# A hybrid encoder layer: another order for the output projection's first loads and the feed-forward's first splits, and up-projection weights moved by 64 bytes

## The chip, the cores and the metric

The kernel runs on one core of a Trainium2 chip. The metric is the device time of one execution in microseconds (us), from the runs of the whole program. A profile is one further execution, taken by the hardware profiler, with a time of its own. The engines are called PE (TensorE, matmuls), DVE (VectorE), ACT (ScalarE), POOL (GpSimd) and SP (SyncE, which here issues the loads). PEld is PE's weight load.

## The reference

One layer (DEPTH = 1) works on x of 512 rows and 1024 columns, all in float32:

```
h      = RMSNorm(x)
parts  = h @ w_in                      # pooling, attention, recurrence and three gates
y_pool = pool_mixer(...)               # 512 x 512 each
y_attn = diff_attention(...)
y_rec  = hgrn2_mixer(...)
merged = sigmoid(gate0) * (y_pool @ w_up_pool[l])
       + sigmoid(gate1) * (y_attn @ w_up_attn[l])
       + sigmoid(gate2) * (y_rec @ w_up_rec[l])
x      = x + merged @ w_out[l]
h2     = RMSNorm(x)
gu     = h2 @ w_ffn_in[l]
x      = x + (silu(gu[..., :2816]) * gu[..., 2816:]) @ w_ffn_out[l]
out    = RMSNorm(x)
```

The change touches the gates and up-projections of the last two branches (pooling, attention), the loads of w_out, and the first columns of w_ffn_in.

## The kernel before

**Products in three terms.** [...] Each weight block is split on the chip into a high part, `whi` (a cast on ACT, L183), and the rest, `wlo` (a subtraction on DVE, L184). The moving operand is split likewise, and a product is hi·hi + lo·hi + hi·lo. `split_w` does this for a block of 128 x 1024 (or 128 x 512) into a buffer of the pool `wsp`, which has three and a little room at the end of each: its argument `skip` puts the block `skip` bytes further on in the buffer.

**Half-size products.** For a pair of column blocks, a form with seven products of half size (256 columns) takes the place of eight: the "pairs". Of their weights, four parts are made: part 0 and part 3 are plain splits of the raw weights (whole, and half), parts 1 and 2 are splits of sums of raw weights. The sums are made by `PairChunk.add` on DVE (L261, L264, L265), their splits by L300 (`shi`, ACT) and L302 (`slo`, DVE). Five pairs of gate blocks (pooling 6, attention 0, 2, 4 and 6) and the pairs 1 to 21 of the feed-forward work this way; the gate pairs' plain parts have `skip=64`. A pair's body has four generators, `first` to `fourth`, one for each part; each issues its matmuls and what takes the results out of PSUM, such as `g` (L1250), `u` (L1255) and `hid` (L1261) in the feed-forward.

**What sets the order.** `Jobs` holds a list of jobs in order, each with its weight parts. `pump` looks ahead: it loads the next chunk of raw weights (about 1 MB, on SP's queue) as soon as fewer than two chunks of the pool `wraw` are still to be split, and splits the next part when fewer than `limit` (3, later 4) parts are held. A chunk with a `where` has a pool of its own instead: it waits until that pool is opened (`Chunk.ready`). `PairPart.ready` and `behind` add an order by hand: a pair's part isn't split before an event named in `after` has been issued, and its instructions stand behind that event's on their engines. The table `after` names events for pairs 1 to 3 alone: `forms_mid` and `forms_end` are points in the making of the moving operand's forms (sums of blocks of h2 and their splits, which need DVE too), `g1` is pair 1's addition into `g`, and `s12_2` is pair 2's first `slo`.

**The stages around the change.** After the pooling mixer come, in order: up-projections of the pooling branch and its gate pair 6; up-projections 6 and 7; attention gate pairs 0 and 2; up-projections 0 to 3; gate pairs 4 and 6; up-projections 4 to 7. Each up-projection of 128 columns has 12 matmuls of 512 columns; two of them share one weight part. Then x is loaded again (L1655, 2 MB), and the output projection begins: two `out_quarter_job`s, each 256 columns of w_out by four blocks of rows in matmuls of 256 columns, and one `out_last_job` with the other 512 columns, in matmuls of 512. The first megabyte of w_out (columns 0 to 255) goes to the pool `wx`, which is opened at L1650 (`LAST["wx"]`), when the gates' pool of forms has been closed. The norm and its transposes are woven in, and the feed-forward starts: pair 1's first part, the plain columns (`u0`, `g0`, L1209 and on), then pairs 1 to 21. In pair 4, two matmuls of 512 columns whose result isn't used stand behind the first part (L1222 and on), one reading its moving operand at the start of the weight buffer, the other 64 bytes further on.

Of the kernel before, what the change touches and what calls it, by code (L numbers as in the profile page):

```python
# [76 lines left out]
def encoder_kernel(ctx: ExitStack, tc: tile.TileContext, x, norm1_g, w_in, pool_w, pool_scale,  # L77
# [7 lines left out]
    def pool(name, bufs=1, **kw):  # L85
        return tc.tile_pool(name=name, bufs=bufs, **kw)
# [62 lines left out]
    LAST, FF = {}, {}  # L149
# [28 lines left out]
    def split_w(view, a, b, wpool=None, skip=0):  # L178

        n, k = a * b, skip // 4  # L180
        hi, lo = ((wpool or wsp).tile([P, n if wpool else 1088], F32R, name=name)[:, k:k + n]
                  .rearrange("p (a b) -> p a b", a=a) for name in ("whi", "wlo"))
        nc.scalar.copy(out=hi, in_=view)  # L183
        LAST["wlo"] = nc.vector.tensor_tensor(out=lo, in0=view, in1=hi.bitcast(F32), op=ALU.subtract).ins  # L184
        return hi, lo
# [46 lines left out]
    jobs = Jobs()  # L232
# [34 lines left out]
    @contextmanager  # L267
    def behind(after):

        with ExitStack() as st:  # L270
            for i in after:
                st.enter_context(tc.issue_after(i))
            yield

    class PairPart:
# [17 lines left out]
        def sums_and_split(self):  # L293
            k = KT // 2
            if self.which in (1, 2):
                if self.chunk.sums is None:
                    self.chunk.add()
                view = self.chunk.sums[:, 2:4] if self.which == 1 else self.chunk.sums[:, 0:2]
                hi = LAST["ws"].tile([P, 2, k * P], F32R, name="shi")
                nc.scalar.copy(out=hi, in_=view)  # L300
                lo = LAST["ws"].tile([P, 2, k * P], F32R, name="slo")
                on_dve = nc.vector.tensor_tensor(out=lo, in0=view, in1=hi.bitcast(F32), op=ALU.subtract).ins  # L302
                FF.setdefault(f"s12_{self.chunk.name}", (on_dve,))
            elif self.which == 0:
                hi, lo = split_w(self.chunk.raw[:, 0], KT, P, None, self.skip)
                hi, lo = (t.rearrange("p k c -> p (k c)").rearrange("p (n x) -> p n x", n=2) for t in (hi, lo))
            else:
                hi, lo = split_w(self.chunk.raw[:, 1, k:], k, P, None, self.skip)
                hi, lo = (t.rearrange("p k c -> p (k c)").rearrange("p (n x) -> p n x", n=1) for t in (hi, lo))
            self.hi, self.lo = (t.rearrange("p n (k c) -> p n k c", c=P) for t in (hi, lo))  # L310
            self.chunk.left -= 1
# [101 lines left out]
    def quarter_parts(w, c0, n, where=None, skip=0):  # L413

        v = w.rearrange("(kt p) c -> p kt c", p=P)
        for c in range(0, n, 256):
            ch = Chunk(v[:, :, c0 + c:c0 + c + 256], KT, 256, where if c == 0 else None)
            yield slice(c, c + 256), [Part(ch, lambda raw, j=j: raw[:, j:j + 4, :], 4, 256, None, skip)
                                       for j in (0, 4)]
# [57 lines left out]
    stA = ExitStack()  # L477
# [213 lines left out]
    def up_job(idx, dt, y, first, last_hl):  # L691
        def body(part):
            ps = bank("mm")
            yield from cols_mm(ps, part, y(), 4, dt % 2)
            sg = gate_sb.pop((idx, dt))
            if first:
                nc.vector.tensor_tensor(out=merged[:, dt, :], in0=ps, in1=sg, op=ALU.mult)
                return
            nc.vector.tensor_tensor(out=sg, in0=ps, in1=sg, op=ALU.mult)
            nc.vector.tensor_tensor(out=merged[:, dt, :], in0=merged[:, dt, :], in1=sg, op=ALU.add)  # L700
            if last_hl:
                hi, lo = last_hl()
                nc.scalar.copy(out=hi[:, dt, :], in_=merged[:, dt, :])
                nc.vector.tensor_tensor(out=lo[:, dt, :], in0=merged[:, dt, :],
                                        in1=hi[:, dt, :].bitcast(F32), op=ALU.subtract)
        return body

    class Branch:
# [14 lines left out]
                for part, body in zip(parts, gate_pair_bodies(self.idx, dt)):  # L723
                    jobs.add([part], body)

        def add_ups(self, dts, need=None):
            for dt in dts:
                if dt % 2 == 0:
                    self.part = next(self.ups)
                body = up_job(self.idx, dt, self.y, self.first, self.last_hl)  # L730
                jobs.add([self.part], needs(need, body) if need else body)

    def needs(event, body):
        def wrapped(*parts):
            yield event
            yield from body(*parts)
        return wrapped


    fronts, sgs = {}, {}  # L740
# [362 lines left out]
    br_pool = Branch(0, lambda: POOL["y"], w_up_pool)  # L1103
# [1 line left out]
    n_mix = len(jobs.jobs)  # L1105
    br_pool.add_ups(range(4))
    br_pool.add_gates(range(4, 6))
    br_pool.add_ups(range(4, 6))
    br_pool.add_gate_pairs((6,))
    br_pool.add_ups(range(6, 8))  # L1110
    n_pool = len(jobs.jobs)
    br_att = Branch(1, lambda: ATT["y"], w_up_attn, last_hl=lambda: LAST["m"])
    br_att.add_gate_pairs((0, 2))
    br_att.add_ups(range(4))
    br_att.add_gate_pairs((4, 6))
    n_gates = len(jobs.jobs)
    br_att.add_ups(range(4, 8))
    n_last = len(jobs.jobs)


# [35 lines left out]
            rows_T(h, OUT["hT"], b, 1, full=OUT["full"])  # L1156
            mark(f"H{b}")

    for cs, parts in quarter_parts(w_out[0], 0, 512, "wx"):
        jobs.add(parts, out_quarter_job(cs, cs.start == 0))  # L1160

    class Late:
# [15 lines left out]
    def hid_of(j):  # L1178
        return FF["hid"][j // 8][:, j % 8, :]
# [33 lines left out]
    def ffn_pair_bodies(j):  # L1213
        c = {}


        def first(part):
            f = FF["forms"]
            c["x"], c["zy"] = bank("mm")[:, 0:256], bank("rc")
            c["u"] = FF["t"].tile([P, S], F32, name="u")  # L1220
            yield from product(c["x"], part, 0, f.r11, True)
            nc.scalar.copy(out=c["u"][:, 0:256], in_=c["x"])  # L1222
            yield from product(c["zy"][:, 0:256], part, 1, f.r21, True)


            if j == 4:
                w = part.hi.rearrange("p n k c -> p (n k c)")
                for skip in (0, 16):
                    mm(bank("tp"), w[:, 0:P], w[:, skip:skip + 512], True, True)

        def second(part):
            f = FF["forms"]
            y = c["y"] = c["zy"][:, 256:]
            if j == 2:
                with behind(FF["s12_2"]):
                    ffn_pair_evac(0, *FF["first"])
            c["g"] = FF["t"].tile([P, S // 2], F32, name="g2")
            yield from product(c["x"], part, 1, f.n2, False)
            nc.scalar.copy(out=c["u"][:, 256:], in_=c["x"])
            yield from product(y, part, 0, f.n1, True)  # L1240
            FF["y1"] = (nc.scalar.copy(out=c["g"], in_=y).ins,)

        def third(part):
            f = FF["forms"]
            if j == 1:
                with behind(FF["forms_end"]):
                    pairs[2][1].chunk.add()
            c["sl"] = FF["t"].tile([P, S], F32, name="silu")
            yield from product(c["x"], part, 0, f.d, False)
            on_dve = nc.vector.tensor_tensor(out=c["g"], in0=c["x"], in1=c["g"], op=ALU.add).ins  # L1250
            if j == 1:
                FF["g1"] = (on_dve,)
            nc.scalar.activation(out=c["sl"][:, 256:], in_=c["g"], func=AF.Silu, scale=-1.0)
            yield from product(c["y"], part, 1, f.r22, False)
            nc.vector.tensor_tensor(out=c["u"], in0=c["u"], in1=c["zy"], op=ALU.add)  # L1255

        def fourth(part):
            f = FF["forms"]
            yield from product(c["x"], part, 0, f.n4, False)
            nc.scalar.activation(out=c["sl"][:, 0:256], in_=c["x"], func=AF.Silu, scale=-1.0)  # L1260
            nc.vector.tensor_tensor(out=hid_of(j), in0=c["sl"], in1=c["u"], op=ALU.mult)  # L1261
            if j == FT - 1:
                for i in range(2):
                    hid_split(i)

        return first, second, third, fourth

    pair_bodies = {j: ffn_pair_bodies(j) for j in range(1, FT)}
    after = {1: (None, None, "forms_mid", "forms_mid"), 2: ("g1",) * 4, 3: ("s12_2",) * 4}
    pairs = {j: pair_parts(j, *ffn_cols(j), after.get(j, (None,) * 4)) for j in range(1, FT)}  # L1270
    plain = PairChunk(*ffn_cols(0))
    plain.where = "pl"
# [374 lines left out]
    stG.close()  # L1647
    del LAST["ws"]
    LAST["wp"] = stM.enter_context(pool("wop", 4, side="right"))
    LAST["wx"] = stA.enter_context(pool("wx"))  # L1650
    pipe.run([jobs.stream(n_last - n_gates)])
    stA.close()

# [82 lines left out]
```

## Time and profile before

| what | value |
|---|---|
| runs, median (lowest to highest of 3) | 889.37 us (889.17 to 890.05) |
| profiled execution, its own time | 896.07 us |
| its span, first to last instruction | 894.3 us |
| granted TensorE clock, mean | 0.999 |
| PE busy | 883.5 us (99%) |
| DVE busy | 658.5 us (74%) |
| ACT busy | 442.6 us (49%) |
| data moved | 88.50 MB, mean 99 GB/s |

In a timeline, a row has the start in us, the busy time, the engine, the line of the kernel, the operation, its output and inputs with shapes, and the number of like instructions that follow one another (x4). In brackets stands the engine's idle time ahead of the row and what released it. Matmuls are pipelined: one of 256 columns lasts about 0.28 us, but the next starts 0.11 to 0.12 us after it, so rates are read from one start to the next, and not from durations. L90 is the line of a helper through which all matmuls go.

### The profile page before, as it was taken

Reading aid. Unit: us, or ns where it says so; the run is one execution under the profiler, and the core shown is the slowest. Engines: PE = TensorE matmul, PEld = TensorE weight load, DVE = VectorE, ACT = ScalarE, POOL = GpSimd, SP = SyncE. Lnnn points to the kernel's source line nnn. Section 1 sums busy time; section 2 is a strip of 40 time slices with the busy share of each in tenths; the row PEclk is TensorE's granted clock in tenths of the full one; section 3 lists DMA queues with packets and bytes.
Section 4 is the critical chain, followed back from the end, with each engine's and each line's share of the span. In section 5 each row is a group of like instructions: output and inputs, shape, how many; then the busy total and the mean of one; then the engine's idle time right before and its main releaser. Section 6 shows DMA issues by size and latency. Waiting matters only on the chain.

```text
span 894.3 us, 13667 instructions
## 1 busy us (share of the span) xinstructions
PE 883.5 (99%) x5542; PEld 791.6 (89%) x5542; DVE 658.5 (74%) x988; ACT 442.6 (49%) x691; POOL 18.9 (2%) x35
## 2 busy tenths in 40 slices
PE   8999999999999999999999999999999999999996
PEld 7989978878998888888999898999999999988885
DVE  6787566844859765788776645998887888846996
ACT  5644343424746584443454334755555555433563
POOL 1000000000000000000000001000000000000001
PEclk9999999999999999999999999999999999999999
DMA  7330113024134114221431760244433433355002
GB/s 239 95 118 24 48 48 117 24 71 136 45 95 139 48 48 153 95 93 48 142 96 48 259 188 1 72 119 125 111 96 96 128 107 95 119 188 177 11 1 94
DMA packets 109578, 88.50 MB, mean 99 GB/s; under 512 B 2742, under 2 KB 98508, under 8 KB 109388
## 3 DMA queue, kind: packets, MB, share of 16 engines
q1 hardware_dynamic: 108924, 86.59, 31.4%
q8 instruction: 43, 0.70, 0.3%
q10 hardware_dynamic: 592, 1.05, 0.3%
q14 instruction: 19, 0.16, 0.1%
HBM read 85.54 MB, written 2.10 MB: 98 GB/s over the span
## 4 chain that ended last, share of the span: by engine, by line
PE 92%; DVE 3%; DMA 2%; issue 1%; ACT 1%; POOL 0%; SPq 0%; POOLq 0%; DVEq 0%; ACTq 0%
PE mm L90 62%; PE rc L90 26%; PE tp L90 2%; PE tp L98 2%; DMA raw<-in_w_out_dram 1%; DMA raw<-in_w_in_dram 1%; DVE wlo L184 1%; DVE hid L354 1%; DVE flo L354 1%; DMA xin<-in_x_dram 0%; DVE hrow L455 0%; DVE h_lo L472 0%; DVE slo L302 0%; DVE sums L261 0%; ACT hrow L449 0%
## 5 line engine op out<-in xcount | busy, mean ns | idle before, releaser
L183 ACT CAST whi<-raw 128x1024 fp32r<-128x1024 f32 (+1 forms) x134 | 128.7, 967 | 141.3 <-PE mm L90 91.3
L184 DVE TENSOR_TENSOR wlo<-raw,whi 128x1024 fp32r<-128x1024 f32 (+1 forms) x134 | 149.0, 1116 | 62.9 <-ACT whi L183 37.9
L90 PE MATMUL mm<-hT_hi,whi 128*128 128x512 f32 (+1 forms) x380 | 92.7, 378 | 0.0
L90 PE MATMUL mm<-hT_hi,wlo 128*128 128x512 f32 (+1 forms) x380 | 92.3, 375 | 0.2 <-DVE wlo L184 0.2
L90 PE MATMUL mm<-hT_lo,whi 128*128 128x512 f32 (+1 forms) x380 | 91.0, 375 | 0.0
L90 PEld LDWEIGHTS mm<-hT_hi,whi 128*128 128x128 f32 x380 | 66.4, 189 | 12.4 <-issue 1.0
L90 PEld LDWEIGHTS mm<-hT_hi,wlo 128*128 128x128 f32 x380 | 66.6, 189 | 11.8 <-DVE wlo L184 0.4
L90 PEld LDWEIGHTS mm<-hT_lo,whi 128*128 128x128 f32 x380 | 66.6, 189 | 11.4
L302 DVE TENSOR_TENSOR slo<-sums,shi 128x1024 fp32r<-128x1024 f32 x52 | 63.2, 1217 | 0.3 <-ACT shi L300 0.3
L300 ACT CAST shi<-sums 128x1024 fp32r<-128x1024 f32 x52 | 54.7, 1051 | 3.4 <-DVE sums L264 2.2
L861 DVE TENSOR_TENSOR kq<-kq,pyr 128x256 f32<-128x256 f32 x56 | 21.5, 420 | 26.2 <-PE rc L90 26.2
L261 DVE TENSOR_TENSOR sums<-raw 128x1024 f32<-128x1024 f32 x26 | 31.7, 1218 | 3.3 <-DMA raw<-in_w_in_dram 3.3
L90 PEld LDWEIGHTS rc<-kq,kc 128*128 128x128 f32 x224 | 30.3, 191 | 2.1 <-issue 0.5
L90 PE MATMUL rc<-kq,kc 128*128 128x128 f32 x224 | 31.6, 284 | 0.0
L983 ACT ACTIVATE s<-s,mx 128x512 f32<-128x512 f32 x32 | 23.1, 721 | 15.6 <-DVE mx L981 15.4
L1250 DVE TENSOR_TENSOR g<-mm,g 128x256 f32<-128x256 f32 x21 | 8.9, 423 | 28.5 <-PE mm L90 28.5
L825 ACT COPY kc<-kq 128x512 f32<-128x512 f32 x28 | 18.6, 665 | 21.3 <-PE rc L90 15.6
L90 PE MATMUL mm<-fhi,slo 128*128 128x256 f32 x168 | 26.8, 282 | 0.5 <-DVE slo L302 0.5
L90 PE MATMUL mm<-fhi,shi 128*128 128x256 f32 x168 | 26.7, 281 | 0.1
L90 PE MATMUL mm<-flo,shi 128*128 128x256 f32 x168 | 26.6, 281 | 0.0
L90 PE MATMUL mm<-y_hi,whi 128*128 128x512 f32 x96 | 26.5, 394 | 0.0
L90 PE MATMUL mm<-y_lo,whi 128*128 128x512 f32 x96 | 26.3, 392 | 0.0
(365 smaller groups left out, 1989.6 us busy)
## 6 DMA issues: line engine op xcount, KB each, us to landing
raw<-in_w_ffn_in_dram SPq DMA_DIRECT2D x44, 512.0 KB, 5.2
raw<-in_w_in_dram SPq DMA_DIRECT2D x34, 512.0 KB, 4.8
raw<-in_w_in_dram SPq DMA_DIRECT2D x13, 1024.0 KB, 5.3
raw<-in_w_ffn_out_dram SPq DMA_DIRECT2D x7, 1024.0 KB, 4.9
raw<-in_w_out_dram SPq DMA_DIRECT2D x4, 1024.0 KB, 9.4
xin<-in_x_dram SPq DMA_DIRECT2D x4, 512.0 KB, 4.1
raw<-in_w_up_rec_dram SPq DMA_DIRECT2D x2, 1024.0 KB
raw<-in_w_up_pool_dram SPq DMA_DIRECT2D x2, 1024.0 KB, 5.0
```

The lines of the kernel that those rows point to most:

```text
L90: i = nc.tensor.matmul(out_, lhsT=lhsT, rhs=rhs, start=start, stop=stop, skip_group_check=chain)
L98: tc.keep_in_program_order(nc.tensor.transpose(out_, in_, idn))
L183: nc.scalar.copy(out=hi, in_=view)
L184: LAST["wlo"] = nc.vector.tensor_tensor(out=lo, in0=view, in1=hi.bitcast(F32), op=ALU.subtract).ins
L261: nc.vector.tensor_tensor(out=strided(sums, 0, [[2 * half, 2], [1, half]]), in0=strided(self.raw, 0, [[3 * half, 2], [1, half]]), in1=stri ...
L300: nc.scalar.copy(out=hi, in_=view)
L302: on_dve = nc.vector.tensor_tensor(out=lo, in0=view, in1=hi.bitcast(F32), op=ALU.subtract).ins
L354: last[0] = form(**kw).ins
L825: nc.scalar.copy(out=strided(kc, 0, [[2 * n, S // (2 * n)], [n, 2], [1, n]]), in_=strided(kq, 2 * S, [[2 * n, S // (2 * n)], [S + n, 2], [ ...
L861: nc.vector.tensor_tensor(out=xv, in0=xv, in1=tv, op=ALU.mult)
L983: nc.scalar.activation(out=s, in_=s, func=AF.Exp, scale=-1.0, bias=mx[:, c:c + 1], accum_out=zz[:, i, c:c + 1])
L1250: on_dve = nc.vector.tensor_tensor(out=c["g"], in0=c["x"], in1=c["g"], op=ALU.add).ins
```

## The change

It has three parts. First, the first chunk of w_out loses its own pool: it takes a buffer of `wraw`, in the ordinary order of chunks, and `LAST["wx"]` is no longer opened. Second, `add_ups` gets a list of up-projections whose weight part is split with `skip = 64`: 4 and 6 of the pooling branch, 2 and 6 of the attention branch. Each such part serves two up-projections (24 matmuls); they are the last ones ahead of gate pair 6 of the pooling branch, ahead of the attention gate pairs 0 and 2, ahead of the gate pairs 4 and 6, and ahead of the output projection. A helper that nothing calls (`needs`) goes. Third, at the start of the feed-forward, pair 2's sums are no longer issued ahead of pair 1's addition into `g` (behind `forms_end`) but after it (behind `g1`); pair 2's last part is split behind pair 2's second `slo` (the new event `s34_2`) instead of behind `g1`, and all parts of pair 3 behind `s34_2` instead of `s12_2`.

```diff
@@ PairPart.sums_and_split
                 FF.setdefault(f"s12_{self.chunk.name}", (on_dve,))
+                if self.which == 2:
+                    FF[f"s34_{self.chunk.name}"] = (on_dve,)
@@ Branch
-        def add_ups(self, dts, need=None):
+        def add_ups(self, dts, skips=()):
             for dt in dts:
                 if dt % 2 == 0:
                     self.part = next(self.ups)
+                    self.part.skip = 64 if dt in skips else 0
                 body = up_job(self.idx, dt, self.y, self.first, self.last_hl)
-                jobs.add([self.part], needs(need, body) if need else body)
+                jobs.add([self.part], body)
-
-    def needs(event, body):
...
     br_pool.add_gates(range(4, 6))
-    br_pool.add_ups(range(4, 6))
+    br_pool.add_ups(range(4, 6), (4,))
     br_pool.add_gate_pairs((6,))
-    br_pool.add_ups(range(6, 8))
+    br_pool.add_ups(range(6, 8), (6,))
     n_pool = len(jobs.jobs)
     br_att = Branch(1, lambda: ATT["y"], w_up_attn, last_hl=lambda: LAST["m"])
     br_att.add_gate_pairs((0, 2))
-    br_att.add_ups(range(4))
+    br_att.add_ups(range(4), (2,))
     br_att.add_gate_pairs((4, 6))
     n_gates = len(jobs.jobs)
-    br_att.add_ups(range(4, 8))
+    br_att.add_ups(range(4, 8), (6,))
...
-    for cs, parts in quarter_parts(w_out[0], 0, 512, "wx"):
+    for cs, parts in quarter_parts(w_out[0], 0, 512):
         jobs.add(parts, out_quarter_job(cs, cs.start == 0))
@@ ffn_pair_bodies
         def third(part):
             f = FF["forms"]
-            if j == 1:
-                with behind(FF["forms_end"]):
-                    pairs[2][1].chunk.add()
             c["sl"] = FF["t"].tile([P, S], F32, name="silu")
             yield from product(c["x"], part, 0, f.d, False)
             on_dve = nc.vector.tensor_tensor(out=c["g"], in0=c["x"], in1=c["g"], op=ALU.add).ins
             if j == 1:
                 FF["g1"] = (on_dve,)
+                with behind(FF["g1"]):
+                    pairs[2][1].chunk.add()
...
-    after = {1: (None, None, "forms_mid", "forms_mid"), 2: ("g1",) * 4, 3: ("s12_2",) * 4}
+    after = {1: (None, None, "forms_mid", "forms_mid"), 2: ("g1",) * 3 + ("s34_2",), 3: ("s34_2",) * 4}
@@ the launch of the stages
     LAST["wp"] = stM.enter_context(pool("wop", 4, side="right"))
-    LAST["wx"] = stA.enter_context(pool("wx"))
     pipe.run([jobs.stream(n_last - n_gates)])
```

More of the change, by code (lines that the diff above doesn't have):

```diff
@@ L729, in add_ups @@
                     self.part = next(self.ups)
+                    self.part.skip = 64 if dt in skips else 0
                 body = up_job(self.idx, dt, self.y, self.first, self.last_hl)
-                jobs.add([self.part], needs(need, body) if need else body)
-    def needs(event, body):
[L734 to L737, printed above, removed]
+                jobs.add([self.part], body)
     fronts, sgs = {}, {}
```

## The prediction

> **What bounds the kernel now.** I read the page first, then the chain of waits, then the timeline around the three places that the diff touches.
>
> ```profile
> span 894.3 us, 13667 instructions
> PE 883.5 (99%) x5542; PEld 791.6 (89%) x5542; DVE 658.5 (74%) x988; ACT 442.6 (49%) x691; POOL 18.9 (2%) x35
> PE 92%; DVE 3%; DMA 2%; issue 1%; ACT 1%; POOL 0%; SPq 0%; POOLq 0%; DVEq 0%; ACTq 0%
> ```
>
> TensorE is busy for 883.5 of 894.3 us, and 92% of the chain that ends last is TensorE itself. So only two things can shorten the run: a wait of TensorE taken away, or matmuls that follow one another more closely. The profiled execution took 896.07 us, 1.8 more than its span; the median of the runs is 889.37, 6.7 lower. I make each sum as a difference in the profiled execution and take it off 889.37; scaling by 889.37/896.07 would change a sum of 4 us by 0.03. For this kernel 0.2% is 1.8 us, about what a measurement can tell from no change.
>
> **Part 1, the output projection's first load.** The timeline around the load, and two rows of the page's DMA issues (the last figure is us to landing):
>
> ```profile
> 477.96 0.69 DVE L184 TENSOR_TENSOR wlo<-raw,whi 128x512 fp32r<-128x512 f32 x1 [0.63 <-ACT whi L183]
> ...
> 488.24 1.23 DVE L184 TENSOR_TENSOR wlo<-raw,whi 128x1024 fp32r<-128x1024 f32 x1 [1.55 <-ACT whi L183]
> ...
> 493.28 0.37 SPq L1655 DMA_DIRECT2D x<-in_x_dram  x1
> 494.69 6.50 SPq L162 DMA_DIRECT2D raw<-in_w_out_dram  x3
> ...
> 499.97 1.07 PE L90 MATMUL mm<-y_hi,whi 128*128 128x512 f32 x4
> ...
> 504.15 2.00 ACT L183 CAST whi<-raw 128x1024 fp32r<-128x1024 f32 x2 [1.92 <-DMA raw<-in_w_out_dram]
> ...
> 505.40 0.63 PE L90 MATMUL mm<-whi,m_hi 128*128 128x256 f32 x4
> ...
> 506.21 0.50 PE L90 MATMUL mm<-whi,m_hi 128*128 128x256 f32 x2 [0.17 <-ACT whi L183]
> ...
> 507.26 0.63 PE L90 MATMUL mm<-wlo,m_hi 128*128 128x256 f32 x4
> ...
> 508.25 0.50 PE L90 MATMUL mm<-wlo,m_hi 128*128 128x256 f32 x2 [0.36 <-DVE wlo L184]
> ...
> 514.40 0.37 SPq L162 DMA_DIRECT2D raw<-in_w_out_dram  x1
> ...
> 529.08 2.00 PE L90 MATMUL mm<-whi,m_hi 128*128 128x512 f32 x8
> ```
> ```profile
> raw<-in_w_in_dram SPq DMA_DIRECT2D x13, 1024.0 KB, 5.3
> raw<-in_w_out_dram SPq DMA_DIRECT2D x4, 1024.0 KB, 9.4
> ```
>
> The first megabyte of w_out is issued at 494.69, behind the 2 MB of x on SP's queue, and the cast of it on ACT can't begin before 504.15, while TensorE wants it from 505.40 on. Four matmuls of this kind take 0.47 us undisturbed (below), but 0.81 pass from 505.40 to 506.21 and 0.99 from 507.26 to 508.25: 0.34 + 0.52 = 0.86 us lost. The bracketed idle times (0.17, 0.36) are smaller because the modelled ends of pipelined matmuls overlap the wait.
>
> After the edit this chunk goes into wraw in the ordinary order. Of the two wraw buffers one comes free with the last split of the last gate pair (477.96 + 0.69 = 478.65), the other with the split at 488.24 + 1.23 = 489.5. So the first w_out chunk leaves at about 479, before x, on an idle queue; at the 9.4 us to landing of the loads of w_out, which ran beside x, it is there by 488.4; at the 5.3 of equal chunks of w_in, by 484.3. Its split then needs one of three wsp buffers, which come free at 494.5 and 500.0, as the last gate pair and the up-projection behind it end; a cast and a subtraction of 1.05 + 1.23 us from 500.0 end at 502.3, ahead of the 505.87 and 507.73 at which the waiting matmuls would start undisturbed. Both waits go: −0.86 us. What is late next: the fourth w_out chunk now follows two others through wraw, and its issue moves from 514.40 to about 518. With 5.3 us of load and 3.3 of casts and subtraction (two of 1.05, one of 1.23) it is split by about 526.5; the matmuls of 529.08 would want it at about 527. That is the thin place: if the load takes the 9.4 us, TensorE waits about 3 us.
>
> **Part 2, the first pairs of the feed-forward.** The timeline from 571 to 588 us:
>
> ```profile
> 573.38 0.62 PE L90 MATMUL rc<-h_hi,slo 128*128 128x256 f32 x4
> ...
> 573.62 0.41 DVE L1250 TENSOR_TENSOR g<-mm,g 128x256 f32<-128x256 f32 x1
> ...
> 574.08 0.53 PEld L90 LDWEIGHTS mm<-fhi,whi 128*128 128x128 f32 x4 [0.29 <-DVE g L1250]
> ...
> 577.40 1.06 ACT L300 CAST shi<-sums 128x1024 fp32r<-128x1024 f32 x1
> ...
> 578.49 1.22 DVE L302 TENSOR_TENSOR slo<-sums,shi 128x1024 fp32r<-128x1024 f32 x1 [0.32 <-ACT shi L300]
> 578.51 0.54 PEld L90 LDWEIGHTS mm<-fhi,shi 128*128 128x128 f32 x4 [0.25 <-ACT shi L300]
> ...
> 579.63 1.22 DVE L184 TENSOR_TENSOR wlo<-raw,whi 128x1024 fp32r<-128x1024 f32 x1
> ...
> 579.76 0.53 PEld L90 LDWEIGHTS mm<-fhi,slo 128*128 128x128 f32 x4 [0.26 <-DVE slo L302]
> ...
> 581.37 0.68 DVE L184 TENSOR_TENSOR wlo<-raw,whi 128x512 fp32r<-128x512 f32 x1
> ...
> 581.97 1.22 DVE L302 TENSOR_TENSOR slo<-sums,shi 128x1024 fp32r<-128x1024 f32 x1
> ...
> 583.24 0.74 PE L90 MATMUL mm<-fhi,slo 128*128 128x256 f32 x4 [0.46 <-DVE slo L302]
> ...
> 583.81 0.64 PE L90 MATMUL rc<-h_hi,shi 128*128 128x256 f32 x4
> ```
>
> Between 573.38 and 583.81 stand 19 groups of four matmuls. At the undisturbed 0.454 us of the groups ahead they would take 8.62 us; they take 10.43, so 1.81 us are lost, in the four waits that the rows name: for g, for the cast shi, and for two subtractions slo.
>
> The edit puts g ahead of pair 2's big addition, so g starts at about 572.7 rather than 573.62 and the first wait (0.29 + restart) goes. Behind it the additions keep their order. Pair 2's last split (0.68 us on DVE, 0.62 on ACT) and both plain splits of pair 3 (1.22 + 0.68 on DVE, about 1.7 on ACT) move behind the second slo. The first slo no longer has the 0.6 us of pair 2's last split ahead of it, but its additions start 0.4 later; the second loses 1.22 + 0.68 = 1.9 us of work ahead of it, and its end goes from 583.19 to between 580.0 and 581.3, where TensorE, no longer delayed, wants it at about 581.5. So the wait of 0.6 us at 583.24 goes wholly or nearly; the middle two shrink or stay. I take 0.9 us gained, bounds 0.5 (the first and half of the last) and 1.5. No row shows the new order. What is late next: pair 2's last split and pair 3's first now begin at about 581 rather than 573 to 579. The former is wanted at about 584, the latter at 585 to 586. DVE needs 1.9 + 1.2 us for them and for pair 3's additions, so this just fits.
>
> **Part 3, 64 bytes.** The same matmul of 256 columns runs at two speeds in this trace. Ahead stand groups of the timelines, with the number of matmuls from one row to the next worked out from the groups between; then counts in equal stretches.
>
> ```profile
> 494.50 1.09 PE L90 MATMUL mm<-y_hi,whi 128*128 128x512 f32 x4
> ...
> 504.50 1.07 PE L90 MATMUL mm<-y_hi,wlo 128*128 128x512 f32 x4
> ```
> ```profile
> 562.79 2.02 PE L90 MATMUL rc<-h_hi,whi 128*128 128x512 f32 x8
> ...
> 568.39 0.62 PE L90 MATMUL mm<-fhi,shi 128*128 128x256 f32 x4
> ```
> ```profile
> 428.66 0.64 PE L90 MATMUL mm<-hT_hi,whi 128*128 128x256 f32 x4
> ...
> 432.43 0.63 PE L90 MATMUL mm<-ghi,slo 128*128 128x256 f32 x4
> ```
> ```profile
> 474.80:494.40 19.60, 19.60 (x169) 1.00 0.02 8
> 509.00:529.00 20.00, 20.00 (x172) 1.00 0.72 206
> ```
> ```profile
> 585.00:599.00 14.00, 14.00 (x121) 14.00 (x120) 13.12 (x17) 9.30 (x15) 0.00 (x0) 1.00 0.46 128
> 600.00:640.00 40.00, 40.00 (x342) 40.00 (x342) 33.01 (x41) 22.56 (x37) 0.00 (x0) 1.00 0.39 108
> 735.00:775.00 40.00, 40.00 (x342) 40.00 (x341) 32.71 (x41) 22.48 (x37) 0.00 (x0) 1.00 0.36 114
> ```
>
> From 568.39 to 573.38 there are 44 matmuls: 113.4 ns each. From 428.66 to 432.43 there are 32: 117.8 ns each, 4.4 ns more, at the same granted clock of 1.00. Nothing waits in either stretch. The counts show that the last gate pairs, the output quarters and the feed-forward from 583.24 up to 775 run at the slow step (40 us hold 40/0.1178 = 340 and the overlap at the edges; at the fast step it would be about 354). Gate pairs that aren't counted here I take as slow like the others. The step changes only where something interrupts the row of equal matmuls, above all at the wait of 583.24, fast before and slow ever after.
>
> The 512-column matmuls show a second thing: 44 of them take 10.00 us (227 ns each) in the up-projection, where by the tile addresses weights and moving operand start at the same place in 256 bytes. The 24 from 562.79 to 568.39, whose weights lie 64 bytes further on, take 5.60 us: 233 ns each. And behind these 24 the 256-column matmuls are fast, while behind the 227 ns ones (428.66, and the quarters from 505.40) they are slow. My reading: starts fall on a fixed raster, the phase at the entry decides the step, and the odd step of the offset products changes that phase. The edit gives this offset to the last 24 up-projection products ahead of each gate run and of the quarters, four times 24 = 96.
>
> Cost: 96 × (233.3 − 227.3) = 0.58 us. Gain, if the phase follows: gate pairs 84 + 168 + 168 and quarters 192, together 612 × 4.42 ns = 2.71 us. Net −2.1 us. Bounds: +0.6 (nothing follows) and −2.1. I take −2.1, by the one block of this kind that the trace has; it is one against the 256-column matmuls ahead of it, which were fast as well.
>
> [...]
>
> **Sum.** −0.86 − 0.9 − 2.1 = −3.9 us, 889.4 − 3.9 = 885.5 us, with the feed-forward slow from somewhere in pairs 1 to 3 on, as now.
>
> **Rivals.**
> A. The feed-forward also stays fast. If the wait of 583.24 is gone, the step that held before it (113.4) may hold to 775: (775.1 − 583.2)/0.1178 = 1,629 matmuls × 4.42 ns = 7.2 us more, 885.5 − 7.2 = 878.3. For it: three earlier restarts (574, 578, 580) kept the fast step. Against it: one remaining wait among pairs 2 to 5, or the pair of 512-column matmuls in pair 4 (L1222 and on), is enough to turn it slow.
> B. The feed-forward stays fast, but the gates and quarters don't: 889.4 − 0.9 − 0.9 + 0.6 − 7.2 = 881.0.
> [...]
> D. Slower: the postponed splits form a backlog on DVE. It decides at the second slo: if that ends no earlier than the 583.19 of now, because pair 2's additions start behind g, then pair 2's last split, pair 3's plain splits and its additions (0.68 + 1.22 + 0.68 + 1.2 = 3.8 us) all stand behind it. From 585 to 599 DVE is busy for 13.12 of 14 us, so the backlog drains at 0.06 us per us and TensorE waits for nearly all of it: 889.4 − 0.9 + 0.6 + 3.8 − 0.9 (g's wait and half of the last) = 892.0. For it: DVE's full rows; against it: 1.9 us of DVE work leave the path ahead of that slo. The late fourth w_out chunk (3 us) would end at the same figure.
>
> **Chances.** Forecast 0.31, A 0.29, B 0.14, C 0.14, D 0.12. A and the forecast are nearly even; the wait may vanish, yet the feed-forward passes several more places that can turn the step, so I keep the forecast. Faster by over 0.2%: forecast + A + B = 0.74; within: 0.14; slower: 0.12. The range runs from A less 0.8 us (the upper bound of part 2, and a little) to C and the edge of D: 877.5 to 890.0. The forecast's own range, with part 2 at its bounds, is 884.9 to 885.9, and up to 888 if only some of the gate runs turn fast.
>
> **What would show it.** Step 1: w_out's first issue stands ahead of x's on SP and the quarters have no bracketed wait at their start; wrong if a wait appears at the last output job. Step 2: DVE runs g, then the additions, and no TensorE wait near 583 is left; wrong if slo or a plain split is still waited for. Step 3: the products ahead of the gates take 0.93 rather than 0.91 us per four, and the gates 0.454 rather than 0.471; wrong if both or neither hold. For A and B, a 40 us stretch of the feed-forward holds about 354 matmuls rather than 342. The forecast as a whole is wrong if the step is set by something other than the products directly ahead.

## The result, and the profile after

The kernel is slower: 897.41 us median of 20 runs (890.33 to 901.62) against 888.88 of 20 before, 1.0% more. The ratio on record, 1.0063 with a 95% interval of 1.004 to 1.0085, lies near that of the means (1.0061). The forecast was 885.5, the range 877.5 to 890.0.

The medians can't be read without one more fact: the runs of both kernels fall in two groups about 7 us apart. Of the kernel before, 16 of these runs lie near 888.7 and 4 between 895.5 and 896.6; of the changed kernel, 7 lie between 890.3 and 891.3 and 13 above 897 (three of these above 900, which no trace shows). So two things happened: within each group the change costs about 2 us, and more runs fall in the upper one. The profiled execution of before (896.07) was one of the upper group, while the median it was set against is of the lower. The profiled execution of the changed kernel took 890.91, in the lower group.

The parts are counted here as in the section on the change: first the load, second the 64 bytes, third the feed-forward. (The prediction has the feed-forward as Part 2 and the 64 bytes as Part 3.) The changed kernel's page, its first lines:

```profile
span 889.1 us, 13666 instructions
PE 877.4 (99%) x5542; PEld 785.1 (88%) x5542; DVE 659.0 (74%) x988; ACT 442.6 (50%) x691; POOL 20.0 (2%) x35
```

What the two groups are shows in equal stretches of the feed-forward (TensorE's busy time and matmuls come first). This is the changed kernel:

```profile
640.00:680.00 40.00, 40.00 (x355) 40.00 (x354) 34.46 (x44) 22.35 (x37) 0.00 (x0) 1.00 0.39 107
```

The first profile of before had 342 matmuls in such a stretch, this one has 355 at the same clock: the feed-forward ran at the fast step, 113.4 ns. Over 1,629 matmuls that is the 7.2 us worked out for rival A. (Two profiles alone don't show that this is what parts the groups; the experiments below do.)

The first part, in the changed kernel's timeline, w_out's loads, the casts of the quarters and TensorE:

```profile
479.47 0.37 SPq L162 DMA_DIRECT2D raw<-in_w_out_dram  x1
```
```profile
490.28 0.37 SPq L162 DMA_DIRECT2D raw<-in_w_out_dram  x1
...
494.06 0.37 SPq L1652 DMA_DIRECT2D x<-in_x_dram  x1
...
502.80 9.08 SPq L162 DMA_DIRECT2D raw<-in_w_out_dram  x2
...
516.46 2.94 ACT L183 CAST whi<-raw 128x1024 fp32r<-128x1024 f32 x3 [5.89 <-DMA raw<-in_w_out_dram]
...
517.66 0.63 PE L90 MATMUL mm<-whi,m_hi 128*128 128x256 f32 x4
...
519.45 0.74 PE L90 MATMUL mm<-whi,m_hi 128*128 128x256 f32 x4 [1.16 <-ACT whi L183]
```

The first two loads stand ahead of x, and the two waits at the start of the quarters are gone. A new one has come at 519.45: 1.79 us pass over four matmuls that need 0.47, so 1.32 us are lost. (In the four traces that have this load and this order of casts, the same wait costs 1.07 to 1.78 us.) Three casts follow one another on ACT from 516.46. The first two belong to the fourth w_out load (issued at 511.5, 4.9 us to landing), and ACT stood idle for 5.89 us until it came; the third belongs to the second quarter, whose raw weights had long landed, and TensorE waits for that one.

The second part, ahead of attention pair 0 and in it:

```profile
439.05 1.09 PE L90 MATMUL mm<-y_hi,whi 128*128 128x512 f32 x4
...
443.71 1.09 PE L90 MATMUL mm<-y_hi,wlo 128*128 128x512 f32 x4
444.64 0.64 PE L90 MATMUL mm<-hT_hi,whi 128*128 128x256 f32 x4
```
```profile
444.70:464.40 19.70, 19.70 (x169) 19.70 (x168) 13.73 (x17) 11.09 (x19) 0.00 (x0) 1.00 0.39 109
```

24 products take 5.59 us, 233 ns each as forecast. The gate pairs behind them hold 169 matmuls in 19.7 us: the slow step, as before.

The third part, the start of the feed-forward:

```profile
574.03 0.42 DVE L1246 TENSOR_TENSOR g<-mm,g 128x256 f32<-128x256 f32 x1 [0.39 <-PE mm L90]
...
579.57 0.53 PEld L90 LDWEIGHTS mm<-fhi,shi 128*128 128x128 f32 x4 [0.20 <-ACT shi L300]
...
580.83 0.53 PEld L90 LDWEIGHTS mm<-fhi,slo 128*128 128x128 f32 x4 [0.26 <-DVE slo L302]
...
582.43 2.42 DVE L184 TENSOR_TENSOR wlo<-raw,whi 128x512 fp32r<-128x512 f32 x3
584.77 1.22 DVE L261 TENSOR_TENSOR sums<-raw 128x1024 f32<-128x1024 f32 x1
...
585.90 0.42 DVE L1246 TENSOR_TENSOR g<-mm,g 128x256 f32<-128x256 f32 x1
...
586.38 0.74 PE L90 MATMUL mm<-fhi,whi 128*128 128x256 f32 x4 [0.72 <-DVE g L1246]
...
591.14 0.74 PE L90 MATMUL mm<-fhi,shi 128*128 128x256 f32 x4 [0.40 <-ACT u L1221]
```

The waits for g at 574 and for slo at 583 are gone. In their place g of pair 2 stands on DVE behind three plain splits and pair 3's large addition, and u of pair 3 on ACT comes late. Summed as time beyond the fast step over the 252 matmuls from the first product of pair 1's second part to pair 4's idle matmuls (only intervals over 121 ns count), the waits are 2.31 us, against 1.79 in the first profile of before. The changed kernel's stretch also begins at the slow step (569.52), which is not part of the change: in its second profile (after_again, below) it begins at the fast one.

### The profile page after: what moved, and what is told of

Same layout as the page of the kernel before. It is cut to its first block, busy times and chain, and to the rows that moved or that the text cites. A ratio compares the mean times of both kernels' runs of the same rounds, so it can differ in the third digit from the quotient of the medians.

```text
span 889.1 us, 13666 instructions
## 1 busy us (share of the span) xinstructions
PE 877.4 (99%) x5542; PEld 785.1 (88%) x5542; DVE 659.0 (74%) x988; ACT 442.6 (50%) x691; POOL 20.0 (2%) x35
## 4 chain that ended last, share of the span: by engine, by line
PE 93%; DMA 2%; DVE 2%; ACT 1%; issue 1%; POOL 0%; SPq 0%; POOLq 0%; ACTq 0%
PE mm L90 62%; PE rc L90 27%; PE tp L90 2%; PE tp L98 2%; DMA raw<-in_w_out_dram 1%; DMA raw<-in_w_in_dram 1%; DVE wlo L184 1%; DMA xin<-in_x_dram 0%; ACT whi L183 0%; ACT shi L300 0%; DVE slo L302 0%; DVE hrow L457 0%; DVE gate L701 0%; DVE sums L261 0%; ACT hrow L451 0%
## 5 line engine op out<-in xcount | busy, mean ns | idle before, releaser
L90 PE MATMUL mm<-y_hi,wlo 128*128 128x512 f32 x96 | 26.1, 392 | 0.0
```

The lines of the kernel that those rows point to most:

```text
L90: i = nc.tensor.matmul(out_, lhsT=lhsT, rhs=rhs, start=start, stop=stop, skip_group_check=chain)
```

## The experiments

The theory was that the two groups are the two steps of the feed-forward, drawn when TensorE restarts after its last wait, and that the three parts have local prices that add up. The rivals were that the groups come from loads, the clock or another stage, that the second part shifts the phase of the feed-forward, or that the first part's new wait does. Each comparison is with runs of the kernel before on the same chip; "lower" and "upper" are the groups.

**The kernel before, once more (b0_again).** No edit.

> The kernel before, unchanged, for a second profile. Theory 1 (two lasting steps of the half-size matmuls in the feed-forward): its runs fall in two groups 7.2 us apart, near 888.7 and 896, and the profile shows 40 us of the feed-forward with 354 matmuls if its own time is near 888.7 or 890, and 342 if it is near 896; the granted clock is the same in both. Rival (the groups come from loads, clock or other stages): the feed-forward holds 342 in a profile of the lower group too, and the 7 us lie elsewhere.

889.05 us, 11 of 11 runs in the lower group, as all 35 of before beside it. The profile is of the lower group:

```profile
640.00:680.00 40.00, 40.00 (x356) 40.00 (x355) 33.15 (x42) 23.30 (x38) 0.00 (x0) 1.00 0.39 108
```

356 matmuls instead of 342, at the same clock. The waits at the start of the feed-forward are the same (1.78 us); only the step after the last of them differs. So the groups are that step. The other traces agree: the 1488 matmuls behind the idle ones of pair 4 take 175.25 us in the three profiles of the upper group (before, p1_cast_first, ffn_splits), and 168.6 to 168.7 us in all fifteen of the lower one.

**Each part alone.** The edits are the three parts of the diff above, one in each kernel.

> Only the first w_out chunk in the ordinary order. Theory 1 (the parts' prices are local): the two waits at the start of the quarters go (-0.86 us), and a wait of about 1.3 us for a cast whi comes in the second quarter, where that cast stands behind two casts that wait for the fourth w_out load; within each group of runs +0.3 to +0.6 us or nothing, the share of fast runs as before (about 4 of 5). Rival (the new wait restarts TensorE and so sets the step of all that follows): the share of fast runs falls to near the changed kernel's (about 1 of 3). My forecast's step (no wait takes their place): -0.9 us.

889.82 (11 runs, all lower) against 889.1: +0.7. The wait at 519.27 is there, 1.35 us by its row:

```profile
517.29 0.63 PE L90 MATMUL mm<-whi,m_hi 128*128 128x256 f32 x4
...
519.27 0.74 PE L90 MATMUL mm<-whi,m_hi 128*128 128x256 f32 x4 [1.35 <-ACT whi L183]
```

The feed-forward has the fast step nonetheless (354 matmuls from 600 to 640 us), so this wait doesn't set it. Between traces the quarters differ by as much as this part costs: they take 22.93 to 23.83 us in the eight traces with the old load (mean 23.33), and 23.55 to 24.58 in the four with the new one and this order of casts (mean 23.99). The difference of the means, 0.65, agrees with the runs.

> Only the 96 up-projection products with weights 64 bytes further on. The forecast's step: gates and quarters run at 113.4 ns, -2.1 us. Theory 1 (the offset products run at 233 ns and hand on the step they found): gates stay at 117.8, +0.6 us within each group of runs, share of fast runs as before. Rival: the offset shifts the phase for the feed-forward as well, and the share of fast runs changes.

Ten lower runs between 888.8 and 890.0, two at 896.2 and 897.4: median 889.44, +0.3 in the lower group. Gate pairs and quarters are not helped: 169 matmuls in 19.6 us.

```profile
445.00:464.60 19.60, 19.60 (x169) 1.00 0.39 108
```

> Only the new order at the start of the feed-forward. The forecast's step: -0.9 us, the wait near 583 gone. Theory 1: the wait near 583 goes, but g of pair 2 (about 586) and u of pair 3 (about 591) are late behind the postponed splits, by 0.9 and 0.6 us; within each group +0.2 to +0.9 us; and as the last restart of TensorE is another one, the share of fast runs falls to about 1 of 3, with a median near 896 to 898. Rival (the share falls by parts 1 or 2): the share stays at 4 of 5 and the median within 1 us of before.

Nine lower runs (889.0 to 890.3), three from 896.4 to 896.7: +0.6 in the lower group. Waits 2.35 us instead of 1.78. With +0.7 and +0.3 this makes 1.6 of the 2.1 us between the lower groups of the two kernels.

**The changed kernel once more (after_again).**

> The changed kernel again, unchanged, beside the kernel before on one chip. Theory 1 (three local prices that add up in the fast group: +0.8 for the load, +0.4 for the 64 bytes, +0.6 for the feed-forward's order): its fast group lies 1.8 to 2.0 us above that of before; each stall restarts TensorE at a step that is a matter of chance, and the changed kernel has more restarts late, so a part of its runs lies 6 to 7 us higher. Rival (the high share of slow runs was a matter of the chip of those runs alone): no run of the changed kernel in the higher group here.

Three runs from 891.3 to 891.7, eight from 897.7 to 898.9; beside it only 3 of 34 of before were upper. So the larger share of upper runs was not that of one chip. But the share of before isn't fixed either: in the next batch, on another chip, 26 of 35 of its runs were upper (below), and in a later batch on that same chip 3 of 28.

**The casts in another order (p1_cast_first).**

```diff
+ cast = nc.scalar.copy(out=hi, in_=view).ins            # split_w; kept with wlo where wpool is None
...
+ with behind(LAST["q4"] if getattr(self.chunk, "last", False) else ()):   # Part.split, fourth w_out load
      self.hi, self.lo = split_w(...)
```

> The load's part alone, and the casts and subtractions of the fourth w_out load issued behind those of the second quarter's second half. Theory 1 (the new wait comes from the order on ACT, not from bandwidth): no wait in the quarters at all, -0.7 to -0.9 us against before, and -1.5 against the load's part alone; the quarters then run at 117.8 throughout, handed on from the gates. Rival (the load itself is too late): the wait moves to the last output job and the time stays near 889.8.

Seven lower runs, 888.1 to 889.1 (median 888.48): −0.6 against the lower runs of before on the same chip, a little less than expected, and −1.3 against the first part alone, which ran on another chip. No wait is left in the quarters; from 505.90 to 528.51 us they take 22.61, against 24.00 with the part alone:

```profile
505.90:528.50 22.60, 22.60 (x193) 1.00 0.62 179
```

The load was early enough; the order on ACT made the wait. Five of the twelve runs were upper, against 3 of 34 of before beside them, though the feed-forward's code is as it was.

**Which edit of the third part (ffn_sums, ffn_splits).** One has the sums behind `g1` and the old table, the other the new table and the sums where they were.

> Of the feed-forward's new order only the first edit: pair 2's sums behind pair 1's g, the splits where they were. Theory 1a (the postponed splits do the harm): the wait for g at 574 goes, the later waits stay, and the stretch from the first product of pair 1's second part to the idle matmuls of pair 4, 30.4 us before in the fast group, takes 30.1 to 30.4. Rival 1b (the later sums do the harm): the waits for shi and slo grow, and it takes 30.7 or more.

> Only the second edit: pair 2's last split and pair 3's splits behind pair 2's second slo, the sums where they were. Theory 1a: the wait of 0.6 us near 583 goes, waits for g of pair 2 and u of pair 3 come (together about 1.4 us less what they displace), and the stretch takes 30.9 to 31.3 us. Rival 1b: 30.1 or less.

The stretch takes 31.20 us with the sums alone (waits 2.61 us), and 31.07 with the splits alone, which ran mostly at the slow step; its waits are 1.64, against 1.42 to 1.79 in the five profiles that have before's order and end the stretch at the slow step. In the lower runs the sums cost 0.7 us (889.64 against 888.92), the splits 0.2 (889.13, four runs). So of the two alone it is the sums' place that does the harm, and my own theory 1a is the one that fell. DVE's last sum for shi, ACT's queue and TensorE in the run with the sums alone:

```profile
576.52 0.68 DVE L264 TENSOR_TENSOR sums<-sums,raw 128x512 f32<-128x512 f32 x1
...
577.67 0.62 ACT L183 CAST whi<-raw 128x512 fp32r<-128x512 f32 x1 [0.58 <-PE rc L90]
...
578.20 1.99 ACT L300 CAST shi<-sums 128x1024 fp32r<-128x1024 f32 x2
...
579.29 0.73 PE L90 MATMUL mm<-fhi,shi 128*128 128x256 f32 x4 [1.25 <-ACT shi L300]
```

A plain cast that waits for PE to release a buffer now stands ahead of shi, whose sums were done at 577.20. In the whole third part that cast is postponed, the sums' wait shrinks, and the waits at 586 and 591 take over; these two come with the postponed splits (the run with the splits alone has them too), so in the whole part both edits have a share. Twelve runs each: two upper with the sums, eight with the splits.

**Sums on POOL (pool_sums).** `eng = nc.gpsimd if self.name in (2, 3) else nc.vector` in `PairChunk.add`.

> The kernel before, with the sums of pairs 2 and 3 of the feed-forward on POOL instead of DVE (2.6 us of DVE work each). Theory 1 (the waits between 574 and 583 come from DVE's full rows): the 1.8 us of waits shrink to under 0.6; if no wait is left behind 570 the feed-forward keeps the fast step of its entry in every run, and the time is 887.2 to 888. Rival (POOL is too slow or holds DVE up): the sums take over 2.5 us for the large one, shi waits for POOL, and the time is 889 or more.

Ten of twelve runs took 890.8 to 892.6, one 899.0, and the profiled one 3134, so its trace tells nothing of the others: slower than before by over 2 us, and why isn't shown.

**What shifts the step (dummies).** Theory 2 is what was left of the prediction's reading: the step is a phase, which matmuls of an odd size can shift. At the head of a gate pair's `first`:

```diff
+ w = part.hi.rearrange("p n k c -> p (n k c)")
+ for n in {(0, 6): (128,), (1, 0): (128, 128), (1, 2): (64,), (1, 4): (384,), (1, 6): (128, 128, 128)}[idx, dt]:
+     mm(bank("tp")[:, 0:n], w[:, 0:P], w[:, 0:n], True, True)
```

> The kernel before with extra matmuls ahead of the gate pairs, whose results aren't used: one of 128 columns ahead of pooling pair 6; two of 128 ahead of attention pair 0; one of 64 between pairs 0 and 2; one of 384 ahead of pair 4; three of 128 ahead of pair 6. Theory 2 (the step is a phase that an odd-sized matmul can shift): at least one of the five places turns to 113.4 ns for the pair behind it, and stays so up to the next odd one. Rival (only a wait of TensorE can change it): all five pairs stay at 117.8. Price of the extra matmuls: 8 of 0.1 to 0.2 us, about +0.9 us; each pair turned fast gives 84 x 4.4 ns = 0.37 us back.

889.87 us, +0.8. A view of stretches of time, one for each of the five pairs in that order (us, busy us, matmuls, clock, DMA share, GB/s):

```profile
429.70:438.80 9.10, 9.10 (x82) 1.00 0.43 118
444.70:454.40 9.70, 9.70 (x84) 1.00 0.41 114
454.90:464.00 9.10, 9.10 (x83) 1.00 0.38 104
475.20:485.00 9.80, 9.80 (x85) 1.00 0.03 11
486.10:495.00 8.90, 8.90 (x81) 1.00 0.01 2
```

Near the edges two matmuls overlap; without them the steps are 9.10/80 = 114, 118, 112, 118 and 113 ns; from one start to the next inside each pair 113.4, 117.8, 113.5, 117.8 and 113.4. One or three of 128 columns, and one of 64, turn the pair fast; two of 128, and one of 384, don't. In none of the five places did TensorE wait for another engine. (The interval behind an extra matmul is longer, 171 to 200 ns, behind all but the one of 384, but both where the step turned and where it didn't.) So the step can be changed without such a wait, and the rival falls. The 64 bytes of the up-projections aren't needed for it.

**Setting the step.** If the groups are the step, setting it late must leave one group. In pair 4, the two idle matmuls are replaced (all with moving operand and weights at the same place), and in the gates kernels one of 128 columns goes ahead of pooling pair 6, attention pairs 0 and 4 and, in three of them, the quarters.

```diff
-    for skip in (0, 16):
-        mm(bank("tp"), w[:, 0:P], w[:, skip:skip + 512], True, True)
+    for n in 6 * (512,) + (128,):        # after_set, gates_fast_set, gates_fast_64
+    for n in 6 * (512,):                 # before_slow_set, gates_set_six
+    for n in 4 * (512,):                 # gates_set_four
+        mm(bank("tp")[:, 0:n], w[:, 0:P], w[:, 0:n], True, True)
```

> The changed kernel, with the two idle matmuls of pair 4 replaced by six of 512 columns (operands at the same place in 256 bytes) and one of 128. Theory 2 (six such matmuls bring TensorE to one phase from either step, the one of 128 moves it to the fast one): every run in one group near 892, 0.9 us above the fast group of the changed kernel (4 x 0.23 us more matmuls), and none near 898. Rival (the upper group is not the feed-forward's step, or the step can't be set): two groups again, near 892 and 899.

Nine runs from 891.5 to 892.6, three at 898.8 to 898.9: mostly, not always. Before beside it: 26 of 35 upper. The profile enters pair 4 slow and leaves it fast.

> The kernel before, with the two idle matmuls of pair 4 replaced by six of 512 columns alone, without one of 128. Theory 2: the phase they leave is the slow one, as ahead of the gate pairs: every run near 896.5 to 897, with 342 matmuls in 40 us of the feed-forward. Rival: most runs near 890, as the kernel before.

The opposite of the expectation: all ten runs from 890.0 to 891.2, on the chip where 26 of 35 of before were upper (895.3 to 896.5). The profile enters pair 4 at 117.8 and leaves it at 113.4. The six weren't one unbroken row: `tp` has two banks, and the fourth and sixth matmul come 331 and 322 ns behind the one ahead, not 227. So what I had taken for a settled phase was a row with two short waits in it.

> The load's part with the casts in the better order, and one extra matmul of 128 columns ahead of pooling pair 6, attention pairs 0 and 4, and the output quarters. Theory 2: all gate pairs and quarters at 113.4 ns, 612 x 4.4 = 2.7 us less, 4 x 0.12 us more: 886.2 in the fast group, 893 in the other, which stays. Rival (the one place that turned with one of 128 columns was chance): the other places stay at 117.8, and the fast group lies at 888 or more.

Four runs from 886.5 to 887.1, eight from 893.7 to 894.5. The gate pairs turned fast (165 matmuls in 18.5 us), the quarters didn't (192 in 22.4):

```profile
474.50:493.00 18.50, 18.50 (x165) 1.00 0.35 116
504.20:526.60 22.40, 22.40 (x192) 1.00 0.63 174
```

> As the one before, and the phase set in pair 4 as well (six matmuls of 512 columns and one of 128). Theory 2: one group near 887.2, 1.0 us above the other's fast group, and none near 893: faster than both kernels in every run. Rival: two groups.

Twelve of twelve from 887.9 to 889.0.

> The gate pairs turned and the phase set in pair 4, as in the run with both, but the extra matmul ahead of the output quarters has 64 columns instead of 128. Theory 2: the quarters run at 113.4 ns (192 x 4.4 = 0.85 us less), 887.5 in one group. Rival: they stay at 117.8 and the time at 888.4.

The quarters stayed at 117.8. Nine runs from 887.9 to 889.1, three at 895: the same setter that gave one group in the run ahead.

> The load's part with the casts in the better order, one extra matmul of 128 columns ahead of three gate runs, none ahead of the quarters, and in pair 4 six matmuls of 512 columns alone. Theory 3 (the waits for their own result bank inside the six restart TensorE at the fast phase): one group near 887.9, none near 895. Rival (one group in the earlier run was chance): a part of the runs near 895.

Two of six runs at 888.3 and 888.9, four at 894.5 to 894.7, so the six don't hold either.

> The same with four of 512 columns, in which one wait for the own result bank remains. Theory 3: one group near 887.3. Rival: the one wait isn't enough, and a part of the runs lies near 894.5.

Eleven of eleven from 887.3 to 888.6, ratio to before 0.998 (0.9967 to 0.9993), 887.58 against 889.16 on the same chip: 0.2% faster than before, and below every run of the changed kernel (890.33 at least, on other chips). The profiled run (888.62) enters pair 4 slow and leaves it fast:

```profile
583.00:597.90 14.90, 14.90 (x129) 1.00 0.48 131
600.00:640.00 40.00, 40.00 (x356) 1.00 0.38 106
```

By theory 3 the wait that four matmuls keep does it. Eleven runs on one chip, with one trace, are thin; why four hold and six don't is open.

## Why the prediction was wrong

**The steps that failed.** All three terms of the sum, −0.86 − 0.9 − 2.1 = −3.9 us, failed: in the lower group the changed kernel is 2.1 us slower. The largest is the −2.1 of the 64 bytes ("if the phase follows"): none of the 612 matmuls that were to become fast did so because of them, and only the cost was left. The other two left out what the change puts in the place of the waits it removes. Beyond that, the feed-forward's step, taken as slow "as now", is not a property of the kernel but falls one way or the other in each run; the sum had nothing for a change in the share of slow runs, and that share makes up the rest of the median's 8.5 us.

**The baseline.** A step failed ahead of these: "I make each sum as a difference in the profiled execution and take it off 889.37". The 6.7 us between profile and median were no overhead of profiling: they were the feed-forward's slow step (342 matmuls in 40 us in that profile, 356 in one at 888.82). The median runs were fast already. So "the feed-forward slow from somewhere in pairs 1 to 3 on, as now" described the exception, and the 7.2 us of A and B were counted a second time. Without them A becomes the forecast itself, 885.5, and B becomes 888.2: no step changes anywhere, the waits' 1.8 us go, and the 96 products cost their 0.6. That is what C stands for in the chances and the range. The forecast's own terms aren't touched by this, as the waits are the same in both groups (1.79 and 1.78 us in the feed-forward). The numbers of before could have told it: 6.7 against 7.2 us.

**The load, −0.86.** The removal was right, and the time of the first load too (479.47 forecast as about 479). The fourth load left earlier than forecast, at 511.5 and not about 518, and was there after 4.9 us. I had named the fourth load as the thin place, but looked for its victim in the last output job. The victim stood on ACT: the second quarter's last cast behind the fourth load's two. The term that was missing is +1.3 us (1.32 in the changed kernel). With the casts turned round the gain is there: 0.6 us in the runs, and the quarters took 1.06 us less than in the first profile of before, both at the slow step.

**The 64 bytes (Part 3 of the prediction), −2.1.** The cost, 0.58 us, was right: from the first gate run to the quarters the changed kernel needs 77.19 us, the one before 76.75, so +0.44 for the 72 products in between. The gain was not: in the four traces with these products all five gate pairs kept the slow step, and so did the quarters up to their first wait in the three of them that have the new load. "Behind these 24 the 256-column matmuls are fast" was a row in which they had been fast ahead of the 24 as well. The upper bound, +0.6, came true. That such products never turn a step is not shown, though. At the feed-forward's entry the step ahead of the same 24 was slow in five of eighteen traces. In two of them it stayed slow behind (569.52 in the changed kernel, 567.88 in p1_cast_first), and in three it turned fast with no wait in between (ffn_sums, gates_fast_64, gates_set_four). This is one of the three, with 117.5 ns from row to row ahead (560.40 to 561.34, eight matmuls) and 113.1 behind (567.41 to 571.03, 32):

```profile
560.40 1.11 PE L90 MATMUL mm<-h_lo,whi 128*128 128x256 f32 x8
561.34 2.03 PE L90 MATMUL rc<-h_hi,whi 128*128 128x512 f32 x8
...
567.41 0.62 PE L90 MATMUL mm<-flo,shi 128*128 128x256 f32 x4
...
571.03 0.62 PE L90 MATMUL rc<-h_hi,shi 128*128 128x256 f32 x4
```

So the reading that something at the entry decides is borne out, by these and by the extra matmuls of odd sizes; that the 64 bytes set it reliably is not, and what decides stays open. The fixed raster of starts in that reading was my own guess, and no run shows it.

**The feed-forward (Part 2 of the prediction), −0.9.** The first and last wait went, as forecast. The loss is +0.5 to +0.6 of waits (1.79 to 2.31, and 1.78 to 2.35 with this part alone). "Its additions start 0.4 later" was the harmful term, sized as nothing: alone it adds 0.8 us of waits, by ACT's queue. And "this just fits" failed: it left g of pair 2 behind 3.6 us of DVE work (2.42 + 1.22), and TensorE lost about 1.0 us there. D named this backlog. Its condition did not come: counted from the entry, the second slo ended at 13.0 us, not at 14.8 as before. The net loss was 0.5 us, not 3.8.

**The sum in the lower group:** +0.16 and +0.44 for the 96 products, +0.37 for the quarters (23.44 to 23.81 us), and +0.87 at the start of the feed-forward (30.40 to 31.27; 0.53 of waits and 76 more matmuls at the slow step, 0.34): 1.8 of 2.1 us between the spans, 887.0 and 889.1. These are two traces, and the quarters' 0.37 and the 0.34 would come out otherwise with another pair. **What moved the median** is the share of upper runs, 13 of 20 and 8 of 11. That its last restart, at 591 instead of 583, draws the slow step more often is argued, not shown: with that order alone 3 of 12 were upper, with its splits alone 8 of 12, and with the turned casts, which leave the feed-forward alone, 5 of 12. The share of before itself went from 0 of 35 to 26 of 35 from batch to batch, and on one chip from 26 of 35 to 3 of 28. So why the changed kernel has more upper runs stays open.

## What to carry to other kernels

When the profiled execution lies several us from the median, find where those us are before taking a difference to the median: count matmuls in equal stretches of both. When a load is moved, look at what its casts stand ahead of in the queue of the engine that makes them, not only at who needs them. One place where two things go together does not tell cause from company: look at what held ahead of it as well.

## What the runs showed of the hardware

In the gate pairs, the quarters and the feed-forward, matmuls of 256 columns followed one another at 113.4 or 117.8 ns, at a granted clock of 1.00 in both, and kept that step through whole stages (40 us of the feed-forward held 342 in the first profile of before, 356 in b0_again). In the first profile of before, the wait at 583.24 changed it from 113.4 to 117.8. With one extra matmul of 128 columns ahead of it, and no wait for another engine, pooling pair 6 ran at 113.4 (dummies), where it ran at 117.8 in the kernel before. The 24 matmuls of 512 columns at the feed-forward's entry handed a fast step on in all thirteen traces that came to them with it, but a slow one in only two of five.

In the up-projections, matmuls of 512 columns took 227 ns (44 in 10.00 us in the first profile of before), and 233 ns where the change moved the weights by 64 bytes (24 in 5.59 us in the changed kernel).

Behind the up-projections' long row of 512-column matmuls the gate pairs were slow in every trace without an extra matmul (in the changed kernel 169 in 19.7 us). In gates_fast, one extra matmul of 128 columns in three gate places made the step fast (165 in 18.5 us; the next matmul came 60 ns behind it, then 173), while in the quarters, with 58 and 171 ns, it stayed slow (192 in 22.4 us). What makes the difference isn't shown: behind the three of 128 columns ahead of attention pair 6 (dummies) the interval was 171 ns too, and the pair was fast at 113.4.
